# Third branch of a decoder layer's mixer: its split input in the second FFN's accumulator places

## The chip, the cores and the metric

The kernel runs on one core of one Trainium2 chip. The metric is the device time of one execution in microseconds (us). TensorE does the matmuls (PE in the rows; PEld are its weight loads), VectorE is DVE, ScalarE is ACT, GpSimd is POOL, SyncE is SP. SP and ACT also issue the DMA transfers, in the order of their instructions (SPq and ACTq are these issuing rows).

## The reference, cut to what matters

One layer at 1024 tokens and width 1024: an FFN half-step, a mixer with three branches, a second FFN half-step, each between RMS norms. Around the change:

```python
merged = (g_a * (y_a @ w_branch[l, 0]) + g_b * (y_b @ w_branch[l, 1])
          + g_c * (y_c @ w_branch[l, 2]))
h = h + rms_norm(merged @ w_out[l], mix_post_g[l])
f2 = swiglu(rms_norm(h, ffn2_pre_g[l]), ffn2_w_in[l], ffn2_w_out[l])
```

The y are 1024 x 512 outputs of the recurrent mixer, of windowed attention (y_b) and of memory attention (y_c); the g are sigmoid gates.

## The kernel before, in words

Everything is kept feature-major, in tiles of 128 features x 512 tokens; the tokens fall into two halves h. A product in full precision is made of three matmuls on split operands (`mm3`, L317 to L319): each operand is a rounded part "hi" and a remainder "lo". ACT makes hi (for weights L254, else L379), DVE makes lo by a subtraction (L256, L380). Weights arrive as `w_raw` over SP's queue (L246), into 5 places, and are split into 8 places of `w_hi` and 8 of `w_lo`.

The branches are multiplied in the order 0, 2, 1 (`BRANCHES`). Branches 0 and 2 run as filling between the blocks of the attention, the third one, y_b, after the last block, in `last_branches`. For each output tile `o` (eight of them), `branch_strip` loads a gate tile `gin` over ACT's queue (L1214), multiplies into a PSUM place `pb`, applies the gate with DVE (L1225) and adds to the merged tile with POOL (L1226). There are four PSUM places under the tag of `pb`, and two gate places in each pool. The second branch in time (number 2) does its first two output tiles half by half: o0 and o1 of half 0, then o0 and o1 of half 1, one `pb` and one 128x512 gate each, and from o2 on both halves together, with the two halves' matmuls alternating in threes. o2 therefore takes the places of the first two of these four, its second place from its fourth matmul on; o3 takes those of the other two in the same way, and o4 those of o2. The third branch goes half by half all through: 16 parts of 12 matmuls.

The input of a branch is loaded and split by `load_y`: eight loads (L1189) and eight splits into 16 tiles. For the third branch the loads go to the pool `quarters` (tag `r2`, 8 places), and the 16 split tiles come from the pool `branch`, which also holds the two gate places:

```python
with self.tc.tile_pool(reuse_waits="tile", name="branch", bufs=2) as pool:
    tile = lambda: pool.tile([P, TH], F32R, tag="y", name="y", bufs=16)
    with self.tc.high_priority(offset=self.urgent):
        y = self.load_y(y_d[BRANCHES[2]], tile, self.res_tile)
```

`quarters` has a tag `acc` too: 16 places of 128 x 512 in which the output projection (`out_projection`, L1353) puts its result, half 0 first; the second FFN works in them later. They are asked for after `last_branches`. The eight `r2` places are filled again, with the residual of half 0 (L637), as soon as DVE has split what lay in them.

Where a pool ends, its memory is given to the next ones, and an instruction that writes into such a place waits for whoever used it. `branch` takes over the memory of the pool `gates`, among others, in whose two places the gates of branches 0 and 2 lie. A scheduler orders the instructions of each engine when the program is built, by priorities and by when it reckons a place to be free; on the chip an engine then goes through its list in that order.

Of the kernel before, what the change touches and what calls it, by code (L numbers as in the profile page):

```python
# [11 lines left out]
F32R = mybir.dt.float32r  # L12
# [5 lines left out]
P = 128  # L18
T = 1024
TH = 512  # L20
# [19 lines left out]
BRANCHES = (0, 2, 1)  # L40
# [160 lines left out]
class Builder:  # L201
# [1117 lines left out]
    def last_branches(self, mg, gate_d, y_d):  # L1319

        merged = self.new_u()
        with self.tc.tile_pool(reuse_waits="tile", name="branch", bufs=2) as pool:
            tile = lambda: pool.tile([P, TH], F32R, tag="y", name="y", bufs=16)
            with self.tc.high_priority(offset=self.urgent):
                y = self.load_y(y_d[BRANCHES[2]], tile, self.res_tile)
            for h in (0, 1):
                for _ in self.branch(BRANCHES[2], y, pool, gate_d, mg, (h,)):
                    pass
                for o in range(KD):

                    last = h == 1 and o == KD - 1
                    hi = self.u_tile()
                    lo = self.qpool.tile([P, TH], F32R, tag="hid", name="hid", bufs=3) if last else self.u_tile()
                    self.split(mg[o][h], hi, lo)
                    merged[o][h] = (hi, lo)
        return merged
# [164 lines left out]
```

## Time and profile before

| | us |
|---|---|
| three runs | 2376.53, 2378.07, 2379.35 |
| median | 2378.07 |
| the profiled execution | 2381.53 |
| its span, from the first instruction to the last | 2379.8 |
| granted TensorE clock over the span | 0.996 |

TensorE is busy for 98% of the span. Times in the rows count from the start of the span; a timeline row gives start, duration, engine, line, what is written from what, the count of equal instructions merged into the row, and in brackets the idle time of the engine before it with what ended it.

### The profile page before, as it was taken

Reading aid. Unit: us, or ns where it says so; the run is one execution under the profiler, and the core shown is the slowest. Engines: PE = TensorE matmul, PEld = TensorE weight load, DVE = VectorE, ACT = ScalarE, POOL = GpSimd, SP = SyncE. Lnnn points to the kernel's source line nnn. Section 1 sums busy time; section 2 is a strip of 40 time slices with the busy share of each in tenths; the row PEclk is TensorE's granted clock in tenths of the full one; section 3 lists DMA queues with packets and bytes.
Section 4 is the critical chain, followed back from the end, with each engine's and each line's share of the span. In section 5 each row is a group of like instructions: output and inputs, shape, how many; then the busy total and the mean of one; then the engine's idle time right before and its main releaser. Section 6 shows DMA issues by size and latency. Waiting matters only on the chain.

```text
span 2379.8 us, 33514 instructions
## 1 busy us (share of the span) xinstructions
PE 2343.9 (98%) x12388; PEld 1916.1 (81%) x12388; DVE 1543.4 (65%) x2584; ACT 891.6 (37%) x1648; POOL 95.5 (4%) x134
## 2 busy tenths in 40 slices
PE   8999999999999999999999999999999999999998
PEld 6788888888888777888868887778888888878888
DVE  6986555655478776894655456475998765564535
ACT  5423333422345444223454455234652233342211
POOL 0000000000000000001310000240000000000000
PEclk9999999999999999999999999999999999999999
DMA  7453222533244325325444324555545432263303
GB/s 277 136 188 121 86 87 80 178 115 106 97 161 142 110 99 189 135 93 175 144 156 153 123 97 150 185 188 166 174 162 183 156 120 82 83 202 100 114 23 107
DMA packets 196195, 323.80 MB, mean 136 GB/s; under 512 B 35360, under 2 KB 65568, under 8 KB 195776
## 3 DMA queue, kind: packets, MB, share of 16 engines
q1 hardware_dynamic: 180000, 294.33, 37.7%
q10 hardware_dynamic: 16032, 27.33, 3.4%
q8 instruction: 98, 1.61, 0.3%
q14 instruction: 65, 0.53, 0.1%
HBM read 231.41 MB, written 89.13 MB: 135 GB/s over the span
## 4 chain that ended last, share of the span: by engine, by line
PE 89%; DVE 5%; DMA 3%; ACT 2%; issue 1%; ACTq 0%; SPq 0%; DVEq 0%
PE po L317 7%; PE po L318 6%; PE po L319 6%; PE px L317 6%; PE px L318 6%; PE px L319 6%; PE pgate L317 4%; PE pgate L319 4%; PE pgate L318 4%; PE pz L317 3%; PE pz L318 3%; PE pz L319 3%; PE pr L319 2%; PE pr L317 2%; PE pr L318 2%; PE pb L318 2%
## 5 line engine op out<-in xcount | busy, mean ns | idle before, releaser
L254 ACT CAST w_hi<-w_raw 128x512 fp32r<-128x512 f32 x544 | 336.6, 621 | 903.0 <-PE po L318 213.1
L256 DVE TENSOR_TENSOR w_lo<-w_raw,w_hi 128x512 fp32r<-128x512 f32 x544 | 381.5, 702 | 183.0 <-ACT w_hi L254 171.7
L317 PE MATMUL po<-u,w_hi 128*128 128x512 f32 (+1 forms) x768 | 285.9, 372 | 0.9 <-DVE acc L627 0.9
L318 PE MATMUL po<-u,w_hi 128*128 128x512 f32 (+1 forms) x768 | 285.3, 372 | 0.0
L319 PE MATMUL po<-u,w_lo 128*128 128x512 f32 (+1 forms) x768 | 285.3, 372 | 0.0
L630 DVE TENSOR_TENSOR acc<-po,acc 128x512 f32<-128x512 f32 (+1 forms) x136 | 89.6, 658 | 162.6 <-PE po L319 162.0
L317 PEld LDWEIGHTS po<-u,w_hi 128*128 128x128 f32 x768 | 144.7, 188 | 26.3 <-DVE acc L627 1.6
L318 PEld LDWEIGHTS po<-u,w_hi 128*128 128x128 f32 x768 | 144.7, 188 | 24.9
L319 PEld LDWEIGHTS po<-u,w_lo 128*128 128x128 f32 x768 | 144.7, 188 | 25.0
L317 PE MATMUL pgate<-u,w_hi 128*128 128x512 f32 x384 | 152.8, 398 | 0.0
L319 PE MATMUL pgate<-u,w_lo 128*128 128x512 f32 x384 | 151.8, 395 | 0.0
L318 PE MATMUL pgate<-u,w_hi 128*128 128x512 f32 x384 | 150.0, 391 | 0.0
L317 PE MATMUL px<-f,w_hi 128*128 128x512 f32 x352 | 137.6, 391 | 3.1 <-ACT u L543 0.9
L317 PE MATMUL px<-u,w_hi 128*128 128x512 f32 x352 | 137.3, 390 | 1.2 <-ACT vm L1110 0.9
L318 PE MATMUL pz<-u,w_hi 128*128 128x512 f32 x352 | 137.2, 390 | 0.2 <-DVE u L380 0.2
L319 PE MATMUL px<-u,w_lo 128*128 128x512 f32 x352 | 137.2, 390 | 0.0
L317 PE MATMUL pz<-u,w_hi 128*128 128x512 f32 x352 | 137.0, 390 | 0.1
L319 PE MATMUL pz<-u,w_lo 128*128 128x512 f32 x352 | 137.0, 389 | 0.0
L318 PE MATMUL px<-u,w_hi 128*128 128x512 f32 x352 | 137.0, 389 | 0.0
L318 PE MATMUL px<-f,w_hi 128*128 128x512 f32 x352 | 136.9, 389 | 0.0
L319 PE MATMUL px<-f,w_lo 128*128 128x512 f32 x352 | 136.9, 389 | 0.0
L389 ACT ACTIVATE sq<-acc 128x512 f32<-128x512 f32 (+1 forms) x104 | 61.0, 598 | 93.2 <-DVE acc L630 75.7
(314 smaller groups left out, 4665.7 us busy)
## 6 DMA issues: line engine op xcount, KB each, us to landing
w_raw<-in_ffn_in SPq DMA_DIRECT2D x220, 256.0 KB
w_raw<-in_win SPq DMA_DIRECT2D x112, 256.0 KB
w_raw<-in_ffn_out SPq DMA_DIRECT2D x104, 256.0 KB
hid_d<-g SPq DMA_DIRECT2D x88, 256.0 KB
hid<-hid_d SPq DMA_DIRECT2D x88, 256.0 KB
gate_d<-gate SPq DMA_DIRECT2D x24, 512.0 KB
pk_d<-pk ACTq DMA_DIRECT2D x4, 2560.0 KB
f<-pk_d SPq DMA_DIRECT2D x16, 640.0 KB
```

Of the source, the lines that this page charges most:

```text
L254: self.nc.scalar.copy(hi, x)
L256: self.nc.vector.tensor_tensor(lo, x, hi.bitcast(F32), ALU.subtract)
L317: mm(out, wh, xh, start=first, stop=False, **kw)
L318: mm(out, wh, xl, start=False, stop=False, **kw)
L319: mm(out, wl, xh, start=False, stop=last, **kw)
L389: nc.scalar.activation(sq, x, ACT.Square)
L630: self.nc.vector.tensor_tensor(out, ps, out, ALU.add)
```

## The change

The 16 split tiles of the third branch take the places of the tag `acc` in `quarters`. The pool `branch` keeps its two gate places alone. Nothing is computed in another way.

```diff
@@ -1322,7 +1322,7 @@
         with self.tc.tile_pool(reuse_waits="tile", name="branch", bufs=2) as pool:
             tile = lambda: pool.tile([P, TH], F32R, tag="y", name="y", bufs=16)
             with self.tc.high_priority(offset=self.urgent):
-                y = self.load_y(y_d[BRANCHES[2]], tile, self.res_tile)
+                y = self.load_y(y_d[BRANCHES[2]], lambda: self.qpool.tile([P, TH], F32R, tag="acc", name="y", bufs=16), self.res_tile)
```

ACT, before, where the third branch's splits begin (`y` are the split tiles, `x_re` the loaded input, `gin` gates; gates with numbers up to 13561 are of the second branch in time, 13664 and 13681 are the third branch's first two; `w_hi_13660` is an operand of the third branch):

```order
L1214 DMA gin_13561<-gate_d_80 128x1024
L254 CAST w_hi_13656<-w_raw_13443 128x512
L254 CAST w_hi_13660<-w_raw_13517 128x512
L379 CAST y_13604<-x_re_13620 128x512
L1214 DMA gin_13664<-gate_d_80 128x512
L379 CAST y_13606<-x_re_13624 128x512
L1214 DMA gin_13681<-gate_d_80 128x512
L379 CAST y_13608<-x_re_13628 128x512
```

And now:

```order
L1214 DMA gin_13314<-gate_d_80 128x512
L379 CAST y_13604<-x_re_13620 128x512
L379 CAST y_13606<-x_re_13624 128x512
L379 CAST y_13608<-x_re_13628 128x512
L1214 DMA gin_13331<-gate_d_80 128x512
L379 CAST y_13610<-x_re_13632 128x512
L1214 DMA gin_13348<-gate_d_80 128x512
L379 CAST y_13612<-x_re_13636 128x512
L254 CAST w_hi_13369<-w_raw_13151 128x512
L379 CAST y_13614<-x_re_13640 128x512
L1214 DMA gin_13377<-gate_d_80 128x1024
```

The eight casts stood behind the operand casts that the end of the second branch releases; they now stand among that branch's first gate loads (13297 to 13348 are the gates of its four half parts, 13377 is the gate of o2). The third branch's first two gates moved forward too, to a place ahead of these rows.

DVE, before, at the start of the second branch (`pb` are its PSUM places):

```order
L1225 SCALAR_TENSOR_TENSOR gin_13297<-gin_13297,pb_13299 128x512
L1225 SCALAR_TENSOR_TENSOR gin_13314<-gin_13314,pb_13316 128x512
L1225 SCALAR_TENSOR_TENSOR gin_13331<-gin_13331,pb_13333 128x512
L256 TENSOR_TENSOR w_lo_13371<-w_raw_13151,w_hi_13369 128x512
L1225 SCALAR_TENSOR_TENSOR gin_13348<-gin_13348,pb_13350 128x512
L256 TENSOR_TENSOR w_lo_13375<-w_raw_13285,w_hi_13373 128x512
```

And now:

```order
L1225 SCALAR_TENSOR_TENSOR gin_13297<-gin_13297,pb_13299 128x512
L380 TENSOR_TENSOR y_13607<-x_re_13624,y_13606 128x512
L1225 SCALAR_TENSOR_TENSOR gin_13314<-gin_13314,pb_13316 128x512
L380 TENSOR_TENSOR y_13609<-x_re_13628,y_13608 128x512
L380 TENSOR_TENSOR y_13611<-x_re_13632,y_13610 128x512
L1225 SCALAR_TENSOR_TENSOR gin_13331<-gin_13331,pb_13333 128x512
L380 TENSOR_TENSOR y_13613<-x_re_13636,y_13612 128x512
L256 TENSOR_TENSOR w_lo_13371<-w_raw_13151,w_hi_13369 128x512
L380 TENSOR_TENSOR y_13615<-x_re_13640,y_13614 128x512
L1225 SCALAR_TENSOR_TENSOR gin_13348<-gin_13348,pb_13350 128x512
L380 TENSOR_TENSOR y_13617<-x_re_13644,y_13616 128x512
```

The eight subtractions moved in between the gates; between the third and the fourth gate there are three subtractions where there was one.

SP, before, in the same stretch (`x_re` from `y1` is the third branch's input):

```order
L1189 DMA x_re_13644<-y1_d_6651 128x512
L1189 DMA x_re_13648<-y1_d_6651 128x512
L246 DMA w_raw_13367<-in_wb 128x512
L246 DMA w_raw_13441<-in_wb 128x512
L246 DMA w_raw_13443<-in_wb 128x512
L246 DMA w_raw_13517<-in_wb 128x512
```

And now (`x_re` from `h1` are the residual's loads, which stood behind the ninth `w_raw` load counted from `w_raw_13367`):

```order
L1189 DMA x_re_13648<-y1_d_6651 128x512
L246 DMA w_raw_13367<-in_wb 128x512
L637 DMA x_re_14408<-h1_78 128x512
L637 DMA x_re_14410<-h1_78 128x512
L637 DMA x_re_14412<-h1_78 128x512
L637 DMA x_re_14414<-h1_78 128x512
L246 DMA w_raw_13441<-in_wb 128x512
L637 DMA x_re_14416<-h1_78 128x512
L637 DMA x_re_14418<-h1_78 128x512
L246 DMA w_raw_13443<-in_wb 128x512
```

Since the input's places are split earlier, the residual's loads moved forward with them, to between the weight loads of the second branch.

## Rows read from the trace of the kernel before

**Rows 1.** The page: span, and the chain that ended last by engine.

```profile
span 2379.8 us, 33514 instructions
...
PE 89%; DVE 5%; DMA 3%; ACT 2%; issue 1%; ACTq 0%; SPq 0%; DVEq 0%
```

**Rows 2.** Timeline of PE: from the second branch's last matmul to the third's end.

```profile
1556.07 0.39 PE L319 MATMUL pb<-u,w_lo 128*128 128x512 f32 x1
1557.50 1.19 PE L317 MATMUL pb<-y,w_hi 128*128 128x512 f32 x4 [1.04 <-ACT y L379]
1560.19 0.50 PE L318 MATMUL pb<-y,w_hi 128*128 128x512 f32 x1 [1.50 <-DVE y L380]
...
1602.94 0.39 PE L317 MATMUL pw<-u,w_hi 128*128 128x512 f32 x1
```

**Rows 3.** Timeline of ACT at the start of the third branch.

```profile
1556.31 0.62 ACT L254 CAST w_hi<-w_raw 128x512 fp32r<-128x512 f32 x1 [4.82 <-PE pb L318]
...
1556.83 3.41 ACT L379 CAST y<-x_re 128x512 fp32r<-128x512 f32 x6
```

**Rows 4.** Timeline of DVE at the start of the third branch.

```profile
1557.10 1.36 DVE L256 TENSOR_TENSOR w_lo<-w_raw,w_hi 128x512 fp32r<-128x512 f32 x1
1558.38 4.77 DVE L380 TENSOR_TENSOR y<-x_re,y 128x512 fp32r<-128x512 f32 x6
```

**Rows 5.** Timeline of PE: o2, o3 and o4 of the second branch.

```profile
1523.90 0.50 PE L317 MATMUL pb<-u,w_hi 128*128 128x512 f32 x1 [0.36 <-DVE gin L1225]
...
1528.80 0.39 PE L317 MATMUL pb<-u,w_hi 128*128 128x512 f32 x1
...
1529.48 0.39 PE L317 MATMUL pb<-u,w_hi 128*128 128x512 f32 x1
...
1534.39 0.50 PE L317 MATMUL pb<-u,w_hi 128*128 128x512 f32 x1
```

**Rows 6.** Timeline of DVE: the second branch's gates, and subtractions beside them.

```profile
1521.83 0.69 DVE L1225 SCALAR_TENSOR_TENSOR gin<-gin,pb 128x512 f32<-128x512 f32 x1 [6.51 <-DMA gin<-gate_d]
...
1526.92 0.69 DVE L1225 SCALAR_TENSOR_TENSOR gin<-gin,pb 128x512 f32<-128x512 f32 x1 [3.07 <-DMA gin<-gate_d]
1527.52 0.68 DVE L256 TENSOR_TENSOR w_lo<-w_raw,w_hi 128x512 fp32r<-128x512 f32 x1
1528.33 0.69 DVE L1225 SCALAR_TENSOR_TENSOR gin<-gin,pb 128x512 f32<-128x512 f32 x1
...
1533.65 1.28 DVE L1225 SCALAR_TENSOR_TENSOR gin<-gin,pb 128x512 f32<-128x512 f32 x2 [2.48 <-DMA gin<-gate_d]
1534.85 1.40 DVE L256 TENSOR_TENSOR w_lo<-w_raw,w_hi 128x512 fp32r<-128x512 f32 x1
```

**Rows 7.** Timeline of POOL in the same stretch.

```profile
1527.68 2.94 POOL L1226 TENSOR_TENSOR u<-u,gin 128x512 f32<-128x512 f32 x2 [2.46 <-DVE gin L1225]
1534.41 2.99 POOL L1226 TENSOR_TENSOR u<-u,gin 128x512 f32<-128x512 f32 x2 [3.79 <-DVE gin L1225]
```

**Rows 8.** Timeline of ACT's queue: gates 1, 3 and that of o2.

```profile
1514.75 0.33 ACTq L1214 DMA_DIRECT2D gin<-gate_d  x1
...
1523.91 0.33 ACTq L1214 DMA_DIRECT2D gin<-gate_d  x1
...
1529.39 0.33 ACTq L1214 DMA_DIRECT2D gin<-gate_d  x1
```

**Rows 9.** Timeline of SP's queue: the third branch's input, and the residual.

```profile
1511.58 10.46 SPq L1189 DMA_DIRECT2D x_re<-y_d  x8
...
1560.17 3.33 SPq L637 DMA_DIRECT2D x_re<-h  x6
```

**Rows 10.** Busy time by stretch: us, five engines (x count), PEclk, DMA share, GB/s.

```profile
1511.50:1522.50 11.00, 11.00 (x50) 9.03 (x49) 4.15 (x7) 1.75 (x3) 0.00 (x0) 1.00 0.74 241
```

**Rows 11.** DMA queues from 1514.8 to 1517.8: packets, MB, share (q1 SP, q10 ACT).

```profile
q1 hardware_dynamic: 450, 0.82, 83.0%
q10 hardware_dynamic: 13, 0.03, 5.4%
```

## The prediction

> **What bounds the kernel now.** I read the page first. The chain that ended last is 89% TensorE [rows 1], so a change pays only where TensorE stands still, and costs only where it makes it stand still. The change touches one place, so I went to TensorE's timeline around the third branch. The second branch's last matmul starts at 1556.07, the third's first at 1557.50 and, after four matmuls that need hi tiles only, there is another hole before 1560.19 [rows 2]. Matmuls without a wait start 0.227 us apart (1528.80 to 1529.48 are three steps [rows 5]). The third branch is 16 x 12 = 192 matmuls, 43.6 us; it occupies 1556.30 to 1602.94 [rows 2], 46.64 us. So **3.06 us** are lost in it: 1.04 and 1.50 named as waits, the rest slow first matmuls after each hole.
>
> Why the two waits: ACT's casts of y run at 1556.83, behind a cast of w_hi that began at 1556.31, when the second branch's last matmuls gave up its place [rows 3]. The loads of y had been issued from 1511.58 on [rows 9], 45 us before. DVE then does a w_lo of 1.36 us before its first subtraction for y at 1558.38 [rows 4].
>
> The second place to look at is where the splits go: the start of the second branch. There TensorE is only just fed. It waited for a gated PSUM place before 1523.90 [rows 5], because the first gate, issued at 1514.75 [rows 8], was used by DVE only at 1521.83, after 6.51 us of idling for the transfer [rows 6]. At 1534.39 (o4) it waited a little too: DVE's gate of o2 came at 1533.65, after the transfer [rows 5, 6].
>
> **The change, part by part.**
>
> *Removed: the hole.* The eight casts and eight subtractions go ahead of the second branch's end. They need the input's loads, issued over 10.46 us from 1511.58 on [rows 9]; these now wait for one more thing, DVE's last split of the second branch's input, because they fall on its memory, which makes them a little later. In the new order the last of the eight casts stands just ahead of the gate of o3, so all splits are done by about 1533, over 20 us before use. What is late next for the third branch: its gates, and these are in early too; its weight operands have been cast well ahead. So -3.06.
>
> *Casts on ACT.* 8 x 0.57 us (six take 3.41 [rows 3]) = 4.6 us between gate loads that mostly wait for POOL. ACT is busy 1.75 of 11 us there [rows 10]. Nothing queued behind them is needed by TensorE within 10 us: 0, and some 0.6 us later issue of a gate at worst, which is inside the bounds below.
>
> *Subtractions on DVE.* Five of them fall into waits for gates and cost nothing (6.51, 3.07 and 2.48 us of idling [rows 6]), one stands between gates 1 and 2, of which the second is waited for as well. Two are not covered: between gate 3 (1526.92) and gate 4 (1528.33) stood one subtraction, now three stand [rows 6]. Gate 4 frees the second place of o3, wanted at 1529.48 [rows 5]. Lower end: three at a pitch of 0.61 (two gates take 1.28 [rows 6]) after 1527.52 put gate 4 at 1529.35 and its end at 1530.04, 0.56 us late. Upper end: POOL's adds run from 1527.68, 1.47 each [rows 7], and a subtraction beside them takes 1.40 instead of 0.68 (1534.85, with POOL at work from 1534.41 [rows 6, 7]); if the second subtraction is held until POOL's first add ends at 1529.15, gate 4 comes at 1530.45 and ends 1.66 us late. I take +1.4, near the upper end, because the row at 1534.85 is the same pair of instructions.
>
> *Residual loads on SP.* Eight loads of 256 KB leave the stretch from 1560.17 on [rows 9] and come to 1522 to 1534, where gates 3 and 4 and that of o2 travel. Gate 3 took 3.01 us from issue (1523.91 [rows 8]) to use; with a burst of input loads issued just before it, gate 1 took 7.08 (1514.75 to 1521.83 [rows 6, 8]). So the delay of gate 3 is between 0 and +4.07. Two more loads than before are ahead of it; at the 241 GB/s of the first burst [rows 10] one takes 1.09 us. I take **+1.1**, one load's time, half of what the two would cost if the gate went strictly behind them. The delay moves gates 3 and 4 together, and TensorE's stall at o3 with them.
>
> [...]
>
> *Gate of o2, then o4.* It is delayed as well (512 KB, issued at 1529.39 [rows 8], used at 1533.65 [rows 6]), but o4 now starts later by the stall at o3. Only what its own transfer loses beyond some 1.4 us counts: 0 to +1.5, taken as 0, and o4's wait of about 0.15 us before 1534.39 goes: -0.15. A slow first matmul after the new stall: +0.1.
>
> *After the third branch.* The accumulator places of half 0 are free when half 0 of the branch is done, some 20 us before the projection writes them; those of half 1 are wanted only after the projection's first half. 0.
>
> Sum: -3.06 + 1.4 + 1.1 - 0.15 + 0.1 = **-0.6 us**, that is 2380.9 against the profiled execution's 2381.53 (span 2379.8 [rows 1]). That execution lies 3.46 above the median of the runs; I take the same difference from the median 2378.07: **2377.5**. About 0.2% (4.8 us) is what a measurement of this kernel can tell from no change, so my forecast is "no change that shows": the hole is closed, and most of it opens again 30 us earlier.
>
> **Rivals.**
>
> 1. *The hole closes and little opens.* Gates aren't slowed by the residual's loads and the subtractions go through at their short pitch: -3.06 + 0.56 - 0.05 = -2.55, so 2375.5. If the first gates even land earlier, since the input's loads start a little later, and no stall comes at o3, some 0.5 of the wait before 1523.90 goes too: -3.6, so 2374.4. For it: each transfer moved is small and POOL may be idle at that moment. Against it: TensorE's margin at o3 is 0.46 us (1529.48 against the end of gate 4 at 1529.02), and the order alone uses more. [...]
> 2. *Slower: the residual's loads hold gate 3 as the burst held gate 1.* +4.07 in place of 1.1: -0.6 + 3.0 = +2.4, so 2380.5, and with 0.4 from the gate of o2 2380.9. The mechanism is one: on TensorE at o3 of the second branch, by DMA backlog. It decides the sign once gate 3 takes over 4.7 us from issue to use (3.01 + 1.1 + 0.6). For it: rows 11. Against it: the loads are held back one by one by DVE's subtractions, so they don't come as one burst.
> 3. *The change doesn't do what it says:* the new places are also held up to the end of the second branch, and y comes as late as now: 2378.1. Against it: the casts stand 30 us earlier in ACT's order, and what lay in these places belonged to attention blocks, whose stored output the loads read from 1511.58 on [rows 9].
>
> **Numbers.** Chances: forecast 0.50 (-2.0 to +0.8), rival 1 0.27, rival 2 0.20, rival 3 0.03. Beyond 4.8 us to the faster side I see nothing in the rows except a gain in the stages behind, 0.04 out of rival 1; to the slower side, stalls at both o3 and o4 that add up to 8 us, 0.06 out of rival 2. So faster 0.04, same 0.90, slower 0.06. The range goes from rival 1's best to rival 2: 2374.4 to 2380.9.
>
> **What would show it.** Right: no idle of TensorE before the first matmul of pb<-y; subtractions of y at 1517 to 1533; a new wait of PE pb L317 for DVE gin L1225, 1 to 3.5 us, near 1529 to 1532; gate 3 from issue to use in about 4 us. Wrong: that wait under 0.7 us (rival 1), over 4 us (rival 2); or y cast after 1550 (rival 3); or a difference in the stages after 1603, which I hold to be moved as a whole.

## The result, and the profile after

The changed kernel took 2383.58 us (median of 15 runs, 2380.19 to 2386.41) beside 2378.42 us for the kernel before (median of 15, 2376.07 to 2380.76): ratio 1.0021, 95% interval 1.0013 to 1.0029, **5.2 us slower** by the medians. Measured once more beside the last experiments it was 1.0010 (1.0001 to 1.0019), 1.8 us. Both say slower; together they put the loss between some 2 and 5 us. The forecast, "no change that shows" at 2377.5 with an upper end of 2380.9, was wrong, and on the other side of zero.

The profiled execution took 2383.22 us (span 2381.5), 1.7 more than that of before. The two are compared over the stretch that the change touches, from the first branch matmul after the attention's last matmul to the first of the output projection, since the stage ahead of it happened to be 1.29 us shorter in the execution after (the stages behind it were 0.31 shorter). That stage differs from execution to execution: over the runs below, A begins anywhere between 1504.35 and 1512.52. I cut it at the third branch's first matmul. Stretch A holds 210 matmuls, 47.67 us at 0.227; stretch B is the third branch, 192 matmuls, 43.58 us.

| | A begins | third branch begins | projection begins | A | B |
|---|---|---|---|---|---|
| before | 1507.53 | 1557.50 | 1602.94 | 49.97 | 45.44 |
| after | 1506.24 | 1559.44 | 1604.94 | 53.20 | 45.50 |

So the changed kernel lost 3.23 us in A, where 1.21 of the hole lay, and gained nothing in B, where the other 1.85 lay: 3.29 us in the two together. What the 5.2 us of the medians hold beyond that isn't located by these two traces. In the page TensorE is again busy for 98% of the span:

```profile
span 2381.5 us, 33522 instructions
...
PE 2344.2 (98%) x12388; PEld 1915.9 (80%) x12388; DVE 1543.9 (65%) x2584; ACT 892.9 (37%) x1648; POOL 96.6 (4%) x134
```

TensorE's waits in 1500 to 1620, after (in all, times, longest; us):

```profile
PE pb L317 <- DVE gin L1225: 3.5, 3, 2.5
PE pw L317 <- DVE gin L1225: 1.3, 1, 1.3
```

No wait for y is left, where there were 1.04 and 1.50 [rows 2]; all are waits for gates. TensorE's timeline shows where (start, duration, idle time before):

```profile
1526.82 0.39 PE L319 MATMUL pb<-u,w_lo 128*128 128x512 f32 x1
1527.92 0.50 PE L317 MATMUL pb<-u,w_hi 128*128 128x512 f32 x1 [0.72 <-DVE gin L1225]
...
1528.49 0.40 PE L319 MATMUL pb<-u,w_lo 128*128 128x512 f32 x1
1531.40 0.80 PE L317 MATMUL pb<-u,w_hi 128*128 128x512 f32 x1 [2.51 <-DVE gin L1225]
1531.99 0.63 PE L318 MATMUL pb<-u,w_hi 128*128 128x512 f32 x1
1532.42 0.63 PE L319 MATMUL pb<-u,w_lo 128*128 128x512 f32 x1
...
1595.27 0.47 PE L317 MATMUL pb<-y,w_hi 128*128 128x512 f32 x1 [0.31 <-DVE gin L1225]
...
1604.94 0.47 PE L317 MATMUL pw<-u,w_hi 128*128 128x512 f32 x1 [1.27 <-DVE gin L1225]
```

The two places of o3 of the second branch come late: 1.10 and 2.91 us between starts in place of 0.227, so 0.88 and 2.68 lost, where the kernel before had no wait at all [rows 5]. Behind the second stop matmuls start 0.43 us apart up to 1534.51. The windows say why (columns as in [rows 10]):

```profile
1526.00:1531.40 5.40, 2.17 (x9) 1.15 (x7) 4.22 (x6) 1.69 (x4) 1.65 (x1) 0.97 0.50 174
1531.40:1534.50 3.10, 3.10 (x7) 2.48 (x8) 3.10 (x4) 0.88 (x2) 1.67 (x1) 0.51 0.95 324
1534.50:1560.00 25.50, 25.50 (x114) 21.12 (x113) 13.68 (x17) 3.03 (x5) 15.19 (x11) 1.00 0.58 187
```

The granted clock was 0.51 for 3.1 us, after 5.4 us in which TensorE had been busy for 2.17. The seven steps from 1531.40 to 1534.51 cost 0.37 + 5 x 0.20 + 0.15 = **1.5 us** more than seven steps of 0.227. In the kernel before, the clock was at 1.00 in and behind the two holes of [rows 2]:

```profile
1556.00:1560.20 4.20, 1.65 (x8) 0.71 (x6) 4.20 (x5) 3.79 (x7) 2.95 (x2) 1.00 0.50 151
1560.20:1562.00 1.80, 1.80 (x8) 1.50 (x9) 1.80 (x4) 0.04 (x1) 0.00 (x0) 1.00 0.58 188
```

After the change, the last two waits (0.47 and 1.43 us between starts beyond the usual step) are at the end of the third branch.

Gates 3 and 4 of the second branch in ACT's queue and on DVE, and SP's queue, after:

```profile
1522.55 0.33 ACTq L1214 DMA_DIRECT2D gin<-gate_d  x1
```

```profile
1527.18 0.69 DVE L1225 SCALAR_TENSOR_TENSOR gin<-gin,pb 128x512 f32<-128x512 f32 x1 [2.41 <-DMA gin<-gate_d]
1527.79 0.69 DVE L380 TENSOR_TENSOR y<-x_re,y 128x512 fp32r<-128x512 f32 x1
1528.39 1.76 DVE L256 TENSOR_TENSOR w_lo<-w_raw,w_hi 128x512 fp32r<-128x512 f32 x1
1530.07 0.68 DVE L380 TENSOR_TENSOR y<-x_re,y 128x512 fp32r<-128x512 f32 x1
1530.67 0.67 DVE L1225 SCALAR_TENSOR_TENSOR gin<-gin,pb 128x512 f32<-128x512 f32 x1
```

```profile
1520.91 6.54 SPq L637 DMA_DIRECT2D x_re<-h  x4
```

Gate 3 took 4.63 us from issue to use (3.01 before [rows 6, 8]), with four residual loads issued just ahead of it and beside it; gate 4 follows gate 3 by 3.49 us instead of 1.41 [rows 6].

### The profile page after: what moved, and what is told of

It reads as the page before. It is cut to its first block, busy times and chain, and to the rows that moved or that the text cites. A ratio compares the mean times of both kernels' runs of the same rounds, so it can differ in the third digit from the quotient of the medians.

```text
span 2381.5 us, 33522 instructions
## 1 busy us (share of the span) xinstructions
PE 2344.2 (98%) x12388; PEld 1915.9 (80%) x12388; DVE 1543.9 (65%) x2584; ACT 892.9 (37%) x1648; POOL 96.6 (4%) x134
## 4 chain that ended last, share of the span: by engine, by line
PE 86%; DVE 6%; DMA 4%; ACT 2%; issue 1%; SPq 0%; POOL 0%; DVEq 0%; ACTq 0%
PE po L317 6%; PE po L318 6%; PE po L319 6%; PE px L317 6%; PE px L318 6%; PE px L319 6%; PE pgate L317 3%; PE pgate L319 3%; PE pgate L318 3%; PE pz L318 3%; PE pz L317 3%; PE pz L319 3%; PE pr L319 2%; PE pr L317 2%; PE pr L318 2%; PE pb L317 2%
```

## The experiments

Theories: **L**, the residual's loads hold gate 3; **O**, DVE's order holds gate 4; **K**, the halved clock (0.51) costs time of its own; and for the end of the third branch **G** (two gate places are too few) against **S** (a loop of engines, below). Run 10 has no edit; all edits but that of run 11 are to the changed kernel. `behind(tc, x, f)` runs f under `tc.issue_after(x.ins)`: what f puts on x's engine is queued behind x. `sent` keeps the load of each weight strip, and `gated` the gate instructions of L1225 in order: 0 to 3 are the second branch's four half parts, then two for each o.

**1. The residual's loads later.**

```diff
-                    post(part, self.residual(h1, part, self.res_tile), pool)
+                    post(part, behind(tc, self.sent["wout", 0], lambda: self.residual(h1, part, self.res_tile)), pool)
```

> The changed kernel with one edit: on SP's queue the eight loads of the residual's first half stand behind the first strip of the output projection (from about 1575 us on) instead of between 1520 and 1535. DVE's, ACT's and TensorE's orders are untouched. Theory L (the residual's loads hold gate 3 of the second branch): gate 3 takes 3.0 to 3.5 us from issue to use instead of 4.63, the second stall at o3 falls from 2.7 to 1.0 - 1.6 us, and the time falls by 1.5 to 3 against the changed kernel, the more if TensorE's clock is then not halved (0.51 in 1531.4:1534.5 in the changed kernel). Theory O (DVE's order of subtractions alone): gate 4 still comes after three subtractions, gate 3 stays near 4.6 us because other loads take the place, the stall stays above 2 us, and the time is within 1 us of the changed kernel's.

Measured: 2380.67 us, ratio to the kernel before 1.0002 (0.9993 to 1.0011). DVE around gate 3, which was issued at 1520.65:

```profile
1523.49 0.69 DVE L1225 SCALAR_TENSOR_TENSOR gin<-gin,pb 128x512 f32<-128x512 f32 x1 [0.62 <-DMA gin<-gate_d]
1524.09 0.68 DVE L380 TENSOR_TENSOR y<-x_re,y 128x512 fp32r<-128x512 f32 x1
1524.69 1.78 DVE L256 TENSOR_TENSOR w_lo<-w_raw,w_hi 128x512 fp32r<-128x512 f32 x1
1526.40 0.68 DVE L380 TENSOR_TENSOR y<-x_re,y 128x512 fp32r<-128x512 f32 x1
1527.01 0.67 DVE L1225 SCALAR_TENSOR_TENSOR gin<-gin,pb 128x512 f32<-128x512 f32 x1
```

Gate 3 takes 2.84 us, so L is right, with a price of 1.8 us on gate 3. Gate 4 still comes 3.52 us behind it: one stop of 1.83 us at o3 is left, a little more than L expected, and O accounts for it. The clock stayed at 1.00 behind that stop. The two stretches take 95.05 us; the changed kernel's take 98.70 and, in the execution of run 10, 97.12.

**2. Three subtractions later.**

```diff
-                self.split(t, *out[h][k])
+                behind(self.tc, self.gated[after[4 * h + k]] if 4 * h + k in after else None, lambda: self.split(t, *out[h][k]))
```

with `after = {5: 5, 6: 7, 7: 9}` for the third branch's input.

> The changed kernel with one edit: the last three of the eight subtractions of y stand on DVE behind later gates of the second branch (its o2, o3, o4), so that between gate 3 and gate 4 only one w_lo stands. The residual's first loads stay early. Theory O: gate 4 follows gate 3 by about 1.4 to 2.2 us instead of 3.5, the second stall at o3 falls from 2.7 to 0.9 - 1.4 us, and with no long stop of TensorE its clock is not halved: 1.5 to 3 us less than the changed kernel. Theory L: gate 3 itself is late (4.6 us from issue to use), so a first stall at o3 of 0.9 us stays whatever stands behind it, and the sum of both stalls falls by under 1.5 us.

Measured: 2381.13 us, 1.0008 (0.9999 to 1.0017). Gate 3 took 4.50 us, gate 4 came 2.88 behind it, the stop was 2.09 us, and the clock fell to 0.51 again (1531.3 to 1534.8). O took 0.6 us off the way from gate 3 to gate 4, less than expected, and the clock part of the expectation missed. The first stop of 0.9 us that L foretold didn't come either. The time tells nothing here: run 10, the changed kernel without an edit, has one stop of 2.09 us at o3 too, and its ratio is 1.0010.

**3. Both.**

> Both edits: the residual's loads behind the first strip of the output projection, and the last three subtractions of y behind later gates. If L and O together are what happens in the second branch, the stalls at o3 sum to under 1 us (3.6 in the changed kernel), TensorE's clock stays at 0.97 or more there, and the time is 4 to 5.5 us below the changed kernel's, that is -1.5 to +1 us against the kernel before. If the stall at o3 came from something else that the moved splits do (the casts on ACT, the input's loads), over 2 us of it stay. The third theory, G (the third branch is paced by its two gate places), expects the kernel still not to gain the full 3.06 us of the closed hole: 1.4 to 2 us of waits stay between 1590 and 1606.

Measured: 2379.16 us, 0.9998 (0.9990 to 1.0007). One stop of 1.31 us, clock 1.00, gate 3 in 2.79 us, gate 4 2.91 behind it. Over the two stretches the kernel is 4.55 us below the changed one (94.15 against 98.70); 1.3 us of wait stay before the projection.

**4. Four gate places in the third branch.**

```diff
-            g = pool.tile([P, T], F32, tag="gate", name="gin", bufs=2)[:, :n]
+            g = pool.tile([P, T], F32, tag="gate", name="gin", bufs=4 if i == BRANCHES[2] else 2)[:, :n]
```

> The changed kernel with one edit: the third branch's gates have four places instead of two (the memory that the splits of y left). Theory G (each gate must wait for a place that DVE and POOL give up two parts earlier, 3.2 us per part against TensorE's 2.73): the wait of 1.43 us before the first matmul of the output projection and the 0.47 before 1595.3 go, and the time falls by 1.5 to 2.5 us against the changed kernel; the stalls at o3 of the second branch and the halved clock stay as they are. Rival: the gates are held by DMA or by POOL's adds, not by their places, and the waits at the end of the third branch stay within 0.4 us of 1.9; no change of the time.

Measured: 2381.86 us, 1.0013 (1.0004 to 1.0022). B fell by 0.8 us to 44.70, less than half of what G asked for; it is nearly as low (44.83 to 44.91) in runs 2, 3 and 5, which leave the gate places alone. And gates with a split between them still came 3.72 us apart (DVE L1225 at 1588.64, 1592.36, 1596.09). G as I put it falls. The rows of the changed kernel show the loop that sets this pitch, one engine behind the other:

```profile
1585.60 0.68 DVE L1225 SCALAR_TENSOR_TENSOR gin<-gin,pb 128x512 f32<-128x512 f32 x1
1586.19 0.69 DVE L256 TENSOR_TENSOR w_lo<-w_raw,w_hi 128x512 fp32r<-128x512 f32 x1
1588.71 0.69 DVE L380 TENSOR_TENSOR u<-u 128x512 fp32r<-128x512 f32 x1 [1.83 <-ACT u L379]
1589.33 0.68 DVE L1225 SCALAR_TENSOR_TENSOR gin<-gin,pb 128x512 f32<-128x512 f32 x1
```

```profile
1586.42 1.60 POOL L1226 TENSOR_TENSOR u<-u,gin 128x512 f32<-128x512 f32 x1 [2.12 <-DVE gin L1225]
```

```profile
1588.06 0.62 ACT L379 CAST u<-u 128x512 fp32r<-128x512 f32 x1 [2.58 <-POOL u L1226]
```

DVE's gate at 1585.60 lets POOL add (1586.42), that lets ACT cast the merged part (1588.06), that lets DVE subtract (1588.71), and the next gate stands behind this subtraction in DVE's list (1589.33): 3.73 us for a part that TensorE makes in 2.73. This became theory S.

**5. Four subtractions later** (`after = {4: 5, 5: 7, 6: 9, 7: 11}`), and the edit of run 1.

> As the kernel with both edits, but four instead of three subtractions of y go behind later gates (o2 to o5), so that between gate 3 and gate 4 of the second branch nothing but one w_lo stands, as in the kernel before. In the kernel with both edits gate 3 came 2.8 us after its issue, but gate 4 still 2.9 us behind gate 3, because one subtraction of y (0.68) let POOL's add begin first and the w_lo then took 1.78 us; 1.3 us of stall were left. Theory O refined (it is not the length of the subtractions but that w_lo falls beside POOL's add): w_lo takes 0.7 us again, gate 4 comes 1.3 to 1.5 us behind gate 3, the stall at o3 is under 0.3 us. Rival: w_lo takes 1.7 us all the same, the stall is 0.6 us or more. Time against the kernel with both edits: -1.0 to -1.4 by the first; waits of 1.4 to 2 us at the end of the third branch stay by either.

Measured: 2377.72 us, 0.9990 (0.9981 to 0.9999).

```profile
1524.55 0.69 DVE L1225 SCALAR_TENSOR_TENSOR gin<-gin,pb 128x512 f32<-128x512 f32 x1 [0.61 <-DMA gin<-gate_d]
1525.15 0.69 DVE L256 TENSOR_TENSOR w_lo<-w_raw,w_hi 128x512 fp32r<-128x512 f32 x1
1526.08 0.69 DVE L1225 SCALAR_TENSOR_TENSOR gin<-gin,pb 128x512 f32<-128x512 f32 x1 [0.24 <-DMA gin<-gate_d]
```

Gate 4 comes 1.53 us behind gate 3 and o3 has no stop; one of 0.51 us came before o4. So over the two stretches the kernel is only 0.56 us below run 3 (93.59 against 94.15), less than the 1.0 to 1.4 expected. In the changed kernel POOL's add began at 1527.95 and lasted 1.65 us, and the w_lo behind it, at 1528.39, took 1.76; here the w_lo began first, at 1525.15 with POOL's add at 1525.32, and took 0.69. So a single subtraction of 0.6 us cost 1.4 in run 3.

**6. The merged splits two gates later** (on DVE only, the rest of the changed kernel as it is).

```diff
-                    self.split(mg[o][h], hi, lo)
+                    behind(self.tc, self.gated[min(o + 2, 7) - 8], lambda: self.split(mg[o][h], hi, lo))
```

> The changed kernel with one edit in the third branch: DVE's subtraction that splits merged part o stands behind the gate of part o + 2 instead of ahead of the gate of part o + 1. Theory S: in the changed kernel gate, POOL's add, ACT's cast, DVE's subtraction and the next gate follow one another, 3.73 us where one split stands between two gates (1585.60 to 1589.33), 3.2 us on the mean against TensorE's 2.73; with the split two gates later a gate no longer waits for the add of the one before, and the waits of 0.47 us (1595.3) and 1.43 us (first matmul of the output projection) go: -1.5 to -1.9 us against the changed kernel. Theory G (the gates' loads, through two places, are the limit): DVE then idles for gin<-gate_d before the gates instead, and over 1 us of the waits stays. The stall at o3 of the second branch (3.6 us in all) and the halved clock stay by both.

Measured: 2379.28 us, 0.9999 (0.9990 to 1.0008). S holds: B is 43.52 us, no stop in it, and the two stretches together are 1.53 us below the changed kernel's (97.17 against 98.70). TensorE waits only where it did at o3 (0.96 and 2.68 us, clock 0.52 behind them):

```profile
PE pb L317 <- DVE gin L1225: 3.3, 2, 2.5
```

**7. Runs 5 and 6 together.**

> The edits of the two runs ahead of it together (the residual's loads later, four subtractions of y later, the merged splits two gates later). If the three causes found so far are all there is, TensorE has no wait over 0.3 us between the second branch's o3 and the output projection, the hole of 3.06 us stays closed, and the time is 2 to 4 us below the kernel before (ratio 0.9985 to 0.999). If waits move on instead, they appear in the third branch as DVE waiting for gin<-gate_d, and the gain is under 2 us.

Measured: **2376.33 us, 0.9987 (0.9978 to 0.9995)**. TensorE has no wait in 1500 to 1620 that the list of waits shows; 0.4 us is lost in both stretches together (91.66 us; 4.15 before, 7.45 after).

**8. As 7, with four gate places.**

> As the run ahead of it, and four gate places in the third branch instead of two. If after the merged splits are moved the loads of the gates are the next limit (a place comes free only when POOL has added), this one has 0.3 to 1.5 us less wait at the end of the third branch than the run ahead; if the loads are not waited for, the two are alike within 0.3 us in their waits.

Measured: **2376.14 us, 0.9984 (0.9975 to 0.9993)**; B 43.52 us again, so the gates' places aren't waited for. By these ratios both are faster than either kernel of the case.

**9. Nine matmuls that nothing reads, ahead of the long stop.**

```diff
+                    (i, o, k, h) == (BRANCHES[1], 3, 0, 1) and self.spare(self.block(w, o2 * 4 + k), y[h][k]);
                     self.mm3(ps[h], self.block(w, o2 * 4 + k), y[h][k], k == 0, k == 3)
```

`spare` issues nine 128x512 matmuls into a PSUM place of another tag.

> The changed kernel with nine matmuls that nothing reads put into TensorE's order ahead of the matmul that waits 2.7 us at o3 of the second branch (into a PSUM place of the attention, which is over by then). They take 9 x 0.227 = 2.04 us of a wait of 2.7 us. Theory K (the clock of TensorE falls because it stood still so long, and costs 1.5 us of its own): the wait shrinks to about 0.6 us, the granted clock stays above 0.9 in the 3 us behind it, the next seven steps between matmuls are 0.227 us and not 0.427, and the time is 1.3 to 1.8 us below the changed kernel's, although more work is done. Rival: the fall comes from something else at that moment (the load of the other engines and of DMA): the clock falls all the same, and the time is the changed kernel's.

Measured: 2380.39 us, 1.0004 (0.9995 to 1.0012). Windows like those of the changed kernel above:

```profile
1526.00:1529.00 3.00, 2.97 (x12) 2.17 (x12) 3.00 (x4) 0.88 (x2) 1.67 (x1) 1.00 0.44 111
1529.00:1532.50 3.50, 3.03 (x14) 2.48 (x14) 3.50 (x5) 1.41 (x3) 1.67 (x1) 1.00 0.92 327
```

The clock stays at 1.00, with the other engines and DMA as busy as in the changed kernel, and the steps behind are 0.23 us: K holds, the rival falls. The nine take 2.04 us, 0.63 us of the stop remains. The two stretches are 1.43 us shorter than in the profile of the changed kernel above (97.27 against 98.70), as K has it, but 0.15 longer than in run 10's execution, whose stops at o3 were shorter from the start; by the medians the time fell by 0.65 us against run 10, within the error of both. So the effect on the clock is shown, a gain in time by such matmuls is not. 0.2 us went back as longer waits at the end of the third branch (B 45.71).

**10. The changed kernel again.**

> The changed kernel once more, beside the run with the nine matmuls: the stalls between the end of the attention and the output projection sum to 7.0 to 7.5 us again (98.3 to 98.7 us from the first matmul of the branches alone to the first of the projection), 3 to 3.5 us more than in the kernel before; the ratio lies at 1.0013 to 1.002.

Measured: 2381.04 us, 1.0010 (1.0001 to 1.0019). The two stretches lose 5.86 us, less than expected (97.12 us, 1.71 more than in the kernel before): this execution had one stop at o3 of 2.09 us and none of the first kind.

```profile
1517.72 0.69 DVE L1225 SCALAR_TENSOR_TENSOR gin<-gin,pb 128x512 f32<-128x512 f32 x1 [3.08 <-DMA gin<-gate_d]
1524.67 0.69 DVE L1225 SCALAR_TENSOR_TENSOR gin<-gin,pb 128x512 f32<-128x512 f32 x1 [2.26 <-DMA gin<-gate_d]
```

These are gates 1 and 3. Gate 3 took 4.48 us from issue to use, nearly as long as in the first profile (4.63), and gate 4 again came 3.51 us behind it. But gate 1 was used 12.15 us after A began, not 13.84 as there, and gate 3, which is issued 2.47 us after gate 1's use in both executions, came earlier with it. Gate 1 was issued 0.84 us earlier in A and took 5.52 us instead of 6.37; why it did is open. The clock fell again:

```profile
1529.00:1532.50 3.50, 3.50 (x9) 2.77 (x10) 3.50 (x5) 0.79 (x2) 1.67 (x2) 0.52 0.98 326
```

**11. The kernel before with the edit of run 6 alone.**

> The kernel before with the edit of the merged splits alone (DVE's subtraction of merged part o behind the gate of part o + 2). Theory S with a cover: in the kernel before the hole of 3 us ahead of the third branch gives its gates a lead, so that TensorE meets them late only once, 0.4 us or less; the edit is worth 0 to 0.4 us here, against 1.5 to 2 in the changed kernel. Rival: the loop of gate, add, cast and subtraction costs the kernel before as much as the changed one, and the edit gains over 1 us here too.

Measured: 2380.48 us, 1.0003 (0.9994 to 1.0012). B is 45.45 us, as without the edit (45.44). The loop costs the kernel before nothing: TensorE's only waits in its third branch are the two of the hole [rows 2], and the hole lets the gates catch up. A, in which nothing was edited, is 0.78 us shorter than in the profile of the kernel before; a stretch can differ by that much between executions.

| | A | B | gate 3, issue to use | gate 4 behind gate 3 | stops at o3 | clock behind |
|---|---|---|---|---|---|---|
| before | 49.97 | 45.44 | 3.01 | 1.41 | none | 1.00 |
| after | 53.20 | 45.50 | 4.63 | 3.49 | 0.88 + 2.68 | 0.51 |
| 1 loads | 49.77 | 45.29 | 2.84 | 3.52 | 1.83 | 1.00 |
| 2 subtractions | 51.67 | 44.87 | 4.50 | 2.88 | 2.09 | 0.51 |
| 3 both | 49.32 | 44.83 | 2.79 | 2.91 | 1.31 | 1.00 |
| 4 four gate places | 53.60 | 44.70 | 5.35 | 3.49 | 1.27 + 2.67 | 0.55 |
| 5 four later, loads | 48.68 | 44.91 | 2.85 | 1.53 | none | 1.00 |
| 6 merged splits | 53.65 | 43.52 | 4.67 | 3.49 | 0.96 + 2.68 | 0.52 |
| 7 all | 48.14 | 43.52 | 2.88 | 1.47 | none | - |
| 8 all, four gate places | 47.80 | 43.52 | 3.10 | 1.62 | none | - |
| 9 nine matmuls | 51.56 | 45.71 | 4.73 | 3.51 | 0.83 + 0.63, beside the nine | 1.00 |
| 10 changed again | 51.61 | 45.51 | 4.48 | 3.51 | 2.09 | 0.52 |

## Why the prediction was wrong

- **The place was right.** The cover of the hole, the moved casts and subtractions, the new wait for DVE gin at o3, its two causes and the end of o4's wait came as written. The wait (2.5 us at its longest, 3.5 in all) lay in the stated 1 to 3.5 us.
- **The step "Removed: the hole ... So -3.06" failed.** Its last link was "What is late next for the third branch: its gates, and these are in early too", and again "After the third branch ... 0". The loads of the gates are early; their use is not. The third branch turns over a part in 3.73 us where a split stands between gates, TensorE in 2.73, and without the hole there are only the four PSUM places to make up for it. The hole's 1.85 us in B came back as 1.9 us of waits further on (0.47 and 1.43). Of 3.06 us 1.1 were gained. Runs 6 and 11 show it: the same edit takes 1.98 us off B where the hole is closed, and nothing where it is open.
- **"A slow first matmul after the new stall: +0.1" was mis-sized: 1.5 us.** I priced the restart from the holes in [rows 2], behind which the clock stayed at 1.00, and didn't ask what a longer stop would do. Run 9 shows that it was the standing still: with the stop filled, the clock stayed at 1.00.
- **Residual loads on SP, +1.1, measured 1.6 to 1.9.** Gate 3 takes 2.79 to 2.88 us without the loads (runs 1, 3, 5, 7) and 4.48 to 4.73 with them (after, runs 2, 9, 10); in two runs it was longer, 3.10 without (run 8) and 5.35 with them (run 4). The 1.1 was my estimate, one load's time at the 241 GB/s of [rows 10], and no run shows why one of the two loads should count; the runs lie above that and below the 4.07 of the other end. [rows 11], on which rival 2 leaned, showed only the first 3 us of gate 1's travel; over all of it, 1514.75 to 1521.80 in the kernel before, ACT's queue had 22.0% of the engines' time and SP's 65.2%.
- **Subtractions on DVE, +1.4 of at most 1.66:** the upper end was right. Gate 4 fell back by 2.08 us behind gate 3, where the text had it 2.12 later. The two ends belong to two orders, w_lo ahead of POOL's add (0.69 us) or behind it (1.76), and 1.4 belongs to neither.
- **Gate of o2, o4:** o4's wait went as foreseen, and some 0.5 us of the wait before 1523.90 went too, which only rival 1 had.

The sum by the two profiles: hole -1.1, o3's stops +3.7 with the slow first matmul, clock +1.5, waits before 1523.90 and at o4 -0.7: +3.4, beside the 3.29 measured there. Rival 2, the slower one, named the mechanism at o3 but made the sign hang on gate 3 alone (4.7 us; it took 4.63). It was two terms outside it, the clock and the third branch's own pace, that took the 3.29 us over its upper end, which lay 2.8 above the median.

## What to carry to other kernels

A hole on the bounding engine is also a lead for whoever feeds it: before its length is booked as a gain, work out the pace of the stage behind it, by the list of each engine in order (here gate, add, cast, subtraction, gate), and compare it with the pace of the engine that will no longer stand still. The restart after a long stop can't be priced from the short stops of the old profile either: behind single stops of 2.09 us the clock fell to 0.51 and 0.52, which cost 1.6 and 1.7 us more, while behind two of 1.21 and 1.67 us with four matmuls between them, longer in sum, it stayed at 1.00. The count "this work fits into idle time" fails at an instruction that takes longer beside another engine's work (w_lo: 1.76 us where it began behind POOL's add, 0.69 ahead of it): there the order was worth more than the length.

## What was not expected of the hardware

- TensorE's granted clock fell to 0.51 to 0.55 behind stops of 2.09 us (runs 2 and 10) and of 2.67 to 2.68 us (after, runs 4 and 6), for some 3 us each, and stayed at 1.00 behind stops of 1.83 us (run 1), 1.31 us (run 3), and the two of 1.21 and 1.67 us in the kernel before. It stayed at 1.00 where nine unread matmuls filled the stop (run 9). The fall came with the restart in the changed kernel and in run 10, and 0.6 to 1.6 us after it in runs 2, 4 and 6.
- The w_lo subtraction on DVE (`w_lo<-w_raw,w_hi`) took 0.69 us where it began ahead of POOL's add (run 5) and 1.76 to 1.78 where it began just behind (after, runs 1, 2 and 10); the gate operation of L1225 (`gin<-gin,pb`) took 0.69 even behind a running add (gate 2 at 1521.41 in the changed kernel, POOL's adds from 1520.84 on).
- The same program's stops at o3 were 3.56 us in one execution and 2.09 in another (after, run 10): gate 1's use differed by 1.69 us within A, and gate 3 with it. A stop in one execution is no measure of an edit; the way from gate 3 to gate 4, 3.49 to 3.52 us in every execution with that order on DVE (after, runs 1, 4, 6, 9, 10), is a better one.
